# A hybrid recurrence and retention block: weight blocks stored in split form, a row moved to GpSimd's queue, and three orders changed

## The chip, the cores and the metric

The kernel runs on one core of one Trainium2 chip. The metric is the device time of one execution in microseconds (us). The core's engines are TensorE (PE in the rows; PEld is its weight load), VectorE (DVE), ScalarE (ACT) and GpSimd (POOL); SyncE (SP) issues most of the DMA transfers. Each engine works through its own queue in order; between the engines semaphores decide.

## The reference, cut to what matters

```python
T = concat(meta[16], x[4096])                     # 1024 wide
h = rmsnorm(T) * norm_gain
x_lru, gate, q, k, v, g = split(h @ w_in)         # 1024, 1024, 512, 512, 1024, 1024
y_lru = rg_lru(causal_conv(x_lru)) * gelu(gate)   # block-diagonal gates, linear scan over time
y_ret = head_norm(retention(rope(q), rope(k), v)) * silu(g)   # 8 heads, chunks of 128
out = rmsnorm(x + concat(y_lru, y_ret) @ w_out) * final_gain  # 4096 x 1024
```

All of it is float32.

## The kernel before, in words

Every float32 operand of a product is split into two float32r parts, hi and lo (`split`, L109 to L112: hi by a pass on ACT, L111, lo by a subtraction on DVE, L112), and a product is three matmuls, hi\*hi, hi\*lo and lo\*hi (`mm3`, L119 to L121). TensorE so has most of the work. The program goes through three parts, and a framework orders each engine's queue from the dependences and a simulated time line of its own: an edit of the program text so moves rows on every engine.

**The LRU part (to about 860 us).** Two passes, one for each half of the channels, each over 9 tiles of time (272, 256, then seven of 512). For a tile, four channel blocks each take two projections, `px` and `pg` (PSUM banks a and b, two buffers each). `block_front` (L544) multiplies px by the row 1/rms, which has been spread over the partitions as the tile `rb` (L553), then convolves and splits. `block_back` (L566) computes two gate products `pgt`, and at L576 `sg = pg * rb`: this reads pg and so frees its PSUM buffer. `sg` has 5 buffers (L574). `tail` (L594) scans, multiplies into sg, and stores sg to DRAM (`ydram`, L606, one store for each 128 positions of time): when that store has landed, the sg buffer is free again. The row 1/rms: `stats` (L486) computes it position by position (POOL rows L76 and L77), and from the third tile of the first pass on the result goes to DRAM as `rrow` (L493, 512 elements of 4 bytes) and comes back as rb (`load_rb`, L511); both are requests on SP's queue. The split x is kept in DRAM as `xs` for the later parts.

**The retention (823 to 2084 us).** Two passes over 32 chunks of 128 positions, each with four of the eight heads. `ret_x(ph, n)` (L166; loads L181) requests a chunk's xhi and xlo into the pool `big` (28 buffers), `front_qk` and `front_v` project, `back_s` and `back_o` compute the chunk's output (scores times mask `sm`, L845; `po` is the output's PSUM tile, L857; `on` its normed copy by ACT, L884). In the second pass `stage_w` (L196) prepares the output weights: for each of 8 row pairs of w_out it forms seven combinations (blocks 1 to 7) and stores each to DRAM (`put`, the tensors `wst`, 256 KB per transfer).

**The out-projection (from 2084 us).** Two sweeps (h = 0 for the LRU half of w_out, h = 1 for the retention half) over 16 pairs of row tiles. A pair (a `Unit`) needs seven products instead of eight, in the order of `ORDER` (L231): blocks 1, 6, 7, 5, 2, 4, 3, into PSUM banks a, b, c, d, a, c, d. `out_w(h, i, g)` (L233) loads a half of a block of weights into a tile of the pool `raws` (6 buffers) and splits it. `operand` forms and splits a pair's inputs (`yraw`, `yop`). `combine` (L311) reads the products: for block 1 ACT copies oa to `u` (L315), for block 7 `h1 = u + oc` (L321), and so on. The first two units run together. In the second sweep `finished` (L358) adds the first sweep's result to h by an accumulating load (L368, on POOL's queue); `added` (L398) then requests the squares for the last RMSNorm on ACT (L386, placed behind an instruction called `mark`) and the root on POOL (L393, L395), and `end` (L406) scales (L412) and stores the rows (L414). The last unit has its own end, `last_tile` (L371).

Of the kernel before, what the change touches and what calls it, by code (L numbers as in the profile page):

```python
# [17 lines left out]
P = 128  # L18
D = 1024
# [14 lines left out]
def hybrid_kernel(ctx: ExitStack, tc: tile.TileContext, xa, x, meta, w_in, w_out,  # L34
# [132 lines left out]
    def ret_x(ph, n):  # L167
        if (ph, n) not in rxs:
# [22 lines left out]

    wst = [[[dpool.tile([P, 2, 512], F32, name=f"wst{h}_{i}_{g}") for g in range(2)] for i in range(8)]
           for h in range(2)]
    hdram = [dpool.tile([P, D], F32, name=f"hdram{n}") for n in range(NT)]

    def stage_w(h, k):  # L196
        r = []
        for kk in (k, k + 4):
            t = raws.tile([P, 2, 512], F32, tag="raw", name="sraw")
            r0 = (8 * h + kk) * P  # L200
            nc.sync.dma_start(out=t, in_=w_out[r0:r0 + P, :].rearrange("p (c d) -> p c d", c=2))
            nc.scalar.activation(t, t, AF.Identity, scale=wsc[:, 8 * h + kk:8 * h + kk + 1])
            r.append(t)
        (b11, b12), (b21, b22) = [(t[:, 0], t[:, 1]) for t in r]

        def put(i, src):
            store.dma_start(out=wst[h][i][k // 2][:, k % 2, :], in_=src)

        put(1, b11)
        put(2, b21)  # L210
        put(3, b22)
        nc.vector.tensor_tensor(b11, b12, b11, op=ALU.subtract)
        put(5, b11)
        nc.vector.tensor_tensor(b12, b22, b12, op=ALU.subtract)
        put(7, b12)
        nc.vector.tensor_tensor(b22, b22, b11, op=ALU.subtract)
        put(6, b22)
        nc.vector.tensor_tensor(b21, b21, b22, op=ALU.subtract)
        put(4, b21)
# [13 lines left out]
    def out_w(h, i, g):  # L233
        if (h, i, g) not in wo:
            raw = raws.tile([P, 2, 512], F32, tag="raw", name="oraw")
            load(raw, wst[h][i][g])
            pool = xwp if i in (3, 4) or (i, g) == (2, 1) else big
            hi = pool.tile([P, 2, 512], F32R, tag="b", name="owh")
            lo = pool.tile([P, 2, 512], F32R, tag="b", name="owl")
            split(raw, hi, lo)  # L240
            wo[h, i, g] = (hi, lo)
        return wo[h, i, g]
# [68 lines left out]
    def combine(u, i):  # L311
        g = u.g
        if i == 1:
            u.u = osp.tile([P, 512], F32, name="u2")
            nc.scalar.copy(out=u.u, in_=g[0])  # L315
            return
# [8 lines left out]
        if late_unit(u):  # L325
# [9 lines left out]
            if i == 4:  # L335
                op = add(x1[:, :512], r1[:, :512], g[2])
                finished(u, 1, g[2])
            else:
                for c in range(2):
                    op = add(x0[:, 512 + 256 * c:768 + 256 * c], r0[:, 512 + 256 * c:768 + 256 * c],  # L340
                             g[3][:, 256 * c:256 * c + 256])
                    square_last(u, c)
                with tc.issue_after(op.ins):
                    end()
                    last_tile(u)
            return op
# [23 lines left out]

    def last_tile(u):  # L371
        t, n, v = u.x[0], u.n[0], u.r[0]
        nc.gpsimd.tensor_scalar(er[:, n:n + 1], es[:, n, 0:1], e2[:, 0:1], D * EPS, op0=ALU.add, op1=ALU.add)
        nc.gpsimd.tensor_tensor(er[:, n:n + 1], er[:, n:n + 1], e2[:, 1:2], op=ALU.add)
        nc.gpsimd.tensor_tensor(er[:, n:n + 1], er[:, n:n + 1], pm_half[:, 0:1], op=ALU.pow)
        nc.vector.tensor_tensor(v, t, gb, op=ALU.mult)
        nc.scalar.activation(v[:, :512], v[:, :512], AF.Identity, scale=er[:, n:n + 1])
        nc.sync.dma_start(out=out[n * P:(n + 1) * P, :512], in_=v[:, :512])
        nc.vector.tensor_scalar(v[:, 512:], v[:, 512:], er[:, n:n + 1], None, op0=ALU.mult)
        nc.sync.dma_start(out=out[n * P:(n + 1) * P, 512:], in_=v[:, 512:])  # L380

# [42 lines left out]
    def sweep():  # L424
# [7 lines left out]
        for s, (u, i, b) in enumerate(steps):  # L432
# [16 lines left out]
            if i == 7 or (i, u.n[0]) == (1, 4):  # L449
                added(u.hi[i], 2 if i == 1 else 0)  # L450
            if i in ((6, 5) if u.n[0] == 4 else (4,)) and not late_unit(u):
# [19 lines left out]
    with ExitStack() as ab:  # L471
# [14 lines left out]
        def stats(i):  # L486
# [5 lines left out]
            if i > 1:  # L492
                store.dma_start(out=rrow[i][0, :T].rearrange("(n p) -> p n", p=P),  # L493
                                in_=rstd[:, tiles[0]:tiles[-1] + 1])

        def load_rb(ph, i):
# [13 lines left out]
            else:  # L510
                nc.sync.dma_start(out=rb[:, :T],  # L511
                                  in_=rrow[i][:, :T].partition_broadcast(P).rearrange("a b c -> a (b c)"))
            return rb
# [52 lines left out]
        def block_back(ph, gw, st, T):  # L566
# [3 lines left out]
            for g in range(2):  # L570
                pgt = psp.tile([P, TB], F32, tag="cd"[g], name="pgt")
                mm3(pgt[:, :T], (gw[0][:, g, b, :], gw[1][:, g, b, :]), (xch[:, :T], xcl[:, :T]), True, True)
                ps.append(pgt)
            sg = tp.tile([P, TB], F32, tag="sg", name="sg", bufs=5)  # L574
            tg = mp.tile([P, TB], F32, tag="tg", name="tg", bufs=1)
# [134 lines left out]
    with ExitStack() as cd:  # L710
# [25 lines left out]
        for ph in range(2):  # L736
# [177 lines left out]
            vm = mv_  # L914
            front_v(cur)
            pkv = psp.tile([P, 2, 2, VD], F32, tag="d", name="pkvm")
            for h in range(4):
# [13 lines left out]
            for n in range(1, NT + 1):  # L931
# [25 lines left out]
                if n == NT - 1:  # L957
                    if ph == 0:
                        ret_x(1, 0)
                    else:  # L960
                        for g in range(2):
                            out_w(0, 7, g)
                back_o(prev)
# [94 lines left out]
```

## Time and profile before

| | |
|---|---|
| median of 3 runs | 2729.64 us (2727.87 to 2732.31) |
| the profiled execution | 2727.1 us |
| its span in the profile | 2725.3 us |
| TensorE busy in it | 2684.6 us (99%) |
| mean granted clock of TensorE | 0.995 |
| instructions | 36837 |

The span is what the profile covers of the execution; 1.8 us lie around it. TensorE leaves 40.7 us of the span idle, 9.5 us of them behind its last matmul. A timeline row reads: start, duration, engine, line, operation, output<-inputs, and in brackets the engine's idle time before it and what ended that. "x4" is the number of like instructions in the row; rows of one engine may overlap a little.

### The profile page before, as it was taken

Reading aid. Unit: us, or ns where it says so; the run is one execution under the profiler, and the core shown is the slowest. Engines: PE = TensorE matmul, PEld = TensorE weight load, DVE = VectorE, ACT = ScalarE, POOL = GpSimd, SP = SyncE. Lnnn points to the kernel's source line nnn. Section 1 sums busy time; section 2 is a strip of 40 time slices with the busy share of each in tenths; the row PEclk is TensorE's granted clock in tenths of the full one; section 3 lists DMA queues with packets and bytes.
Section 4 is the critical chain, followed back from the end, with each engine's and each line's share of the span. In section 5 each row is a group of like instructions: output and inputs, shape, how many; then the busy total and the mean of one; then the engine's idle time right before and its main releaser. Section 6 shows DMA issues by size and latency. Waiting matters only on the chain.

```text
span 2725.3 us, 36837 instructions
## 1 busy us (share of the span) xinstructions
PE 2684.6 (99%) x12950; PEld 2259.4 (83%) x12950; DVE 2047.0 (75%) x4553; ACT 1252.5 (46%) x2304; POOL 318.8 (12%) x619
## 2 busy tenths in 40 slices
PE   9999999999999999999999999999999999999998
PEld 8788889888887888888888888888887788887887
DVE  7787789676678877777779887888778755566665
ACT  7676667444454433333335444444334322244443
POOL 1010000000001111111111111111111101012222
PEclk9999999999999999999999999999999999999999
DMA  7765666423245333333335434444323745476664
GB/s 241 221 194 169 207 172 196 143 89 137 103 122 163 100 97 95 102 102 95 102 86 161 119 105 124 135 135 151 82 62 113 176 109 109 110 207 166 176 160 124
DMA packets 433695, 372.03 MB, mean 137 GB/s; under 512 B 160307, under 2 KB 363477, under 8 KB 432997
## 3 DMA queue, kind: packets, MB, share of 16 engines
q1 hardware_dynamic: 420260, 321.44, 38.8%
q0 software_dynamic: 13248, 48.24, 8.6%
q8 instruction: 101, 1.65, 0.3%
q14 instruction: 86, 0.70, 0.1%
HBM read 254.11 MB, written 132.27 MB: 142 GB/s over the span
## 4 chain that ended last, share of the span: by engine, by line
PE 81%; DVE 8%; DMA 6%; issue 2%; ACT 2%; SPq 1%; POOL 0%; POOLq 0%; DVEq 0%; ACTq 0%
PE ps L121 12%; PE ps L119 12%; PE ps L120 12%; PE px L120 3%; PE px L121 3%; PE pg L119 3%; PE pg L120 3%; PE pg L121 3%; PE px L119 3%; DMA ydram<-sg 3%; PE po L857 2%; PE od L308 2%; PE oc L308 2%; PE od L306 2%; PE od L307 2%
## 5 line engine op out<-in xcount | busy, mean ns | idle before, releaser
L121 PE MATMUL ps<-cwh,xlo 128*128 128x512 f32 x1536 | 600.0, 391 | 3.0 <-DMA xlo<-xs 3.0
L120 PE MATMUL ps<-cwl,xhi 128*128 128x512 f32 x1536 | 600.0, 391 | 0.0
L119 PE MATMUL ps<-cwh,xhi 128*128 128x512 f32 x1536 | 599.6, 390 | 0.0
L121 PEld LDWEIGHTS ps<-cwh,xlo 128*128 128x128 f32 x1536 | 288.8, 188 | 64.9 <-DMA xlo<-xs 3.4
L119 PEld LDWEIGHTS ps<-cwh,xhi 128*128 128x128 f32 x1536 | 289.1, 188 | 57.0
L120 PEld LDWEIGHTS ps<-cwl,xhi 128*128 128x128 f32 x1536 | 288.6, 188 | 56.2 <-issue 0.2
L725 DVE STREAM_TRANSPOSE pT<-rd 32x128 f32<-32x128 f32 x1024 | 310.1, 303 | 16.4
L119 PE MATMUL pg<-xhi,lwh 128*128 128x512 f32 (+2 forms) x576 | 212.2, 368 | 6.5 <-DVE sg L576 6.2
L119 PE MATMUL px<-xhi,lwh 128*128 128x512 f32 (+2 forms) x576 | 213.3, 370 | 3.1 <-DVE xlb L553 2.6
L120 PE MATMUL px<-xlo,lwh 128*128 128x512 f32 (+2 forms) x576 | 213.1, 370 | 2.2 <-DMA xlo<-xs 1.2
L121 PE MATMUL px<-xhi,lwl 128*128 128x512 f32 (+2 forms) x576 | 212.8, 370 | 0.2 <-DVE lwl L112 0.2
L121 PE MATMUL pg<-xhi,lwl 128*128 128x512 f32 (+2 forms) x576 | 211.5, 367 | 0.0
L120 PE MATMUL pg<-xlo,lwh 128*128 128x512 f32 (+2 forms) x576 | 211.5, 367 | 0.0
L111 ACT ACTIVATE yop<-yraw 128x512 fp32r<-128x512 f32 x192 | 117.9, 628 | 194.6 <-PE od L308 70.7
L112 DVE TENSOR_TENSOR yop<-yraw,yop 128x512 fp32r<-128x512 f32 x192 | 130.7, 688 | 68.1 <-ACT yop L111 66.4
L559 DVE SCALAR_TENSOR_TENSOR xc<-xlb,vec,xc 128x512 f32<-128x512 f32 (+2 forms) x216 | 149.0, 690 | 21.7 <-ACT xc L556 18.4
L884 ACT ACTIVATE on<-po,nb,rs 128x128 f32<-128x128 f32 x256 | 96.5, 458 | 141.6 <-POOL nb L881 141.6
L119 PEld LDWEIGHTS pg<-xhi,lwh 128*128 128x128 f32 x576 | 108.8, 189 | 25.6 <-DVE sg L576 7.6
L825 DVE SCALAR_TENSOR_TENSOR gs<-th,gs 128x512 f32<-128x512 f32 x64 | 44.2, 691 | 112.4 <-ACT gs L824 112.3
L120 PEld LDWEIGHTS px<-xlo,lwh 128*128 128x128 f32 x576 | 109.2, 190 | 22.9 <-DVE xlo L114 2.5
L119 PEld LDWEIGHTS px<-xhi,lwh 128*128 128x128 f32 x576 | 109.2, 190 | 22.0 <-issue 2.8
L121 PEld LDWEIGHTS px<-xhi,lwl 128*128 128x128 f32 x576 | 109.3, 190 | 18.9 <-DVE lwl L112 0.4
(218 smaller groups left out, 5743.1 us busy)
## 6 DMA issues: line engine op xcount, KB each, us to landing
xhi<-xs SPq DMA_DIRECT2D x92, 512.0 KB, 4.5
xlo<-xs SPq DMA_DIRECT2D x92, 512.0 KB, 5.5
xn<-in_x_dram SPq DMA_DIRECT2D x32, 512.0 KB, 5.3
ydram<-sg SPq DMA_DIRECT2D x256, 64.0 KB, 1.7
hdram<-in_x_dram SPq DMA_DIRECT2D x32, 512.0 KB
yret<-yt SPq DMA_DIRECT2D x256, 64.0 KB, 2.2
yraw<-ydram SPq DMA_DIRECT2D x32, 512.0 KB, 3.3
hdram<-h POOLq DMA_DIRECT2D x32, 512.0 KB, 5.5
```

The costliest lines, as they stand in the source:

```text
L111: hi_op[0] = nc.scalar.activation(hi, src, AF.Identity)
L112: return nc.vector.tensor_tensor(lo, src, hi.bitcast(F32), op=ALU.subtract)
L119: nc.tensor.matmul(ps, ah, bh, start=start, stop=False)
L120: nc.tensor.matmul(ps, ah, bl, start=False, stop=False)
L121: nc.tensor.matmul(ps, al, bh, start=False, stop=stop)
L306: nc.tensor.matmul(o, ah, bh, start=k == 0 and not more, stop=False, skip_group_check=more)
L307: nc.tensor.matmul(o, ah, bl, start=False, stop=False, skip_group_check=more)
L308: mm = nc.tensor.matmul(o, al, bh, start=False, stop=k == 3, skip_group_check=more)
L559: conv = nc.vector.scalar_tensor_tensor(xc[:, :T], xl[:, j:j + T], vec[:, 6 + j, ch:ch + 1], xc[:, :T], op0=ALU.mult, op1=ALU.add)
L725: ins = nc.vector.transpose(dst[32 * g:32 * g + 32, :, 32 * q:32 * q + 32], sv[32 * q:32 * q + 32, :, g, :])
L857: nc.tensor.matmul(po[:, h, :], sm[:, h, :], v[:, h * VD:(h + 1) * VD], start=False, stop=(j == 1))
L884: nc.scalar.activation(on[:, h, :], po[:, h, :], AF.Identity, bias=nb[:, h:h + 1], scale=rs[:, h:h + 1])
```

## The change

Six edits.

1. Blocks 7 and 5 (`PRE`; the third and fourth products) are split in `stage_w` by a pass on ACT and one on DVE for each of 16 pieces of 128x512, and stored as hi and lo, 512 KB a store where it was 256 KB. `out_w` loads hi and lo of these blocks straight into the tiles of weights, so their 8 splits of 128x1024 in the sweeps go. At the last chunk of the retention the request for block 7's weights is joined by that for block 5's.
2. The store of `rrow` (7) and the loads of `rb` (16) go from SP's queue to POOL's.
3. `sg` has 6 buffers, not 5.
4. `ret_x(ph, 1)` is called earlier, ahead of the first chunk's kv product, in both passes.
5. In `added`, the mark behind which the first squares of the second sweep stand is the copy of u by ACT, not the split of the operand of block 1.
6. For the last unit the root of its second tile is computed with its own two instructions, r1 = x1\*gb and half of r0 = x0\*gb are formed before the last product is there, and the new `last_tiles` scales and stores both tiles (four stores on SP).

```diff
-    wst = [[[dpool.tile([P, 2, 512], F32, name=f"wst{h}_{i}_{g}") for g in range(2)] for i in range(8)]
+    PRE = (7, 5)
+    wst = [[[dpool.tile([P, 2 if i in PRE else 1, 2, 512], F32, name=f"wst{h}_{i}_{g}") for g in range(2)] for i in range(8)]
...
         def put(i, src):
-            store.dma_start(out=wst[h][i][k // 2][:, k % 2, :], in_=src)
+            dst = wst[h][i][k // 2][:, :, k % 2, :]
+            if i in PRE:
+                t = raws.tile([P, 2, 512], F32R, tag="raw", name="swp")
+                split(src, t[:, 0], t[:, 1])
+                store.dma_start(out=dst, in_=t.bitcast(F32))
+            else:
+                store.dma_start(out=dst[:, 0], in_=src)
...
     def out_w(h, i, g):
...
-            split(raw, hi, lo)
+            if i in PRE:
+                for s, t in enumerate((hi, lo)):
+                    load(t.bitcast(F32), w[:, s])
+            else:
+                raw = raws.tile([P, 2, 512], F32, tag="raw", name="oraw")
+                load(raw, w[:, 0])
+                split(raw, hi, lo)
...
-            nc.scalar.copy(out=u.u, in_=g[0])
+            u.cp = nc.scalar.copy(out=u.u, in_=g[0])
...
                 op = add(x1[:, :512], r1[:, :512], g[2])
-                finished(u, 1, g[2])
+                square(u, 1, 0, g[2])
+                q = er[:, u.n[1]:u.n[1] + 1]
+                nc.gpsimd.tensor_scalar(q, es[:, u.n[1], 0:1], es[:, u.n[1], 1:2], D * EPS, op0=ALU.add, op1=ALU.add)
+                nc.gpsimd.tensor_tensor(q, q, pm_half[:, 0:1], op=ALU.pow)
+                with tc.issue_after(op.ins):
+                    nc.vector.tensor_tensor(r1, x1, gb, op=ALU.mult)
+                    nc.vector.tensor_tensor(r0[:, :512], x0[:, :512], gb[:, :512], op=ALU.mult)
...
-                    end()
-                    last_tile(u)
+                    last_tiles(u)
...
+    def last_tiles(u):
+        n0, n1 = u.n
+        q0, q1 = er[:, n0:n0 + 1], er[:, n1:n1 + 1]
+        v0, v1 = u.r
+        nc.vector.tensor_tensor(v0[:, 512:], u.x[0][:, 512:], gb[:, 512:], op=ALU.mult)
+        nc.gpsimd.tensor_scalar(q0, es[:, n0, 0:1], e2[:, 0:1], D * EPS, op0=ALU.add, op1=ALU.add)
+        nc.gpsimd.tensor_tensor(q0, q0, e2[:, 1:2], op=ALU.add)
+        nc.gpsimd.tensor_tensor(q0, q0, pm_half[:, 0:1], op=ALU.pow)
+        for n, v, q in ((n1, v1, q1), (n0, v0, q0)):
+            nc.scalar.activation(v[:, :512], v[:, :512], AF.Identity, scale=q)
+            nc.sync.dma_start(out=out[n * P:(n + 1) * P, :512], in_=v[:, :512])
+            nc.vector.tensor_scalar(v[:, 512:], v[:, 512:], q, None, op0=ALU.mult)
+            nc.sync.dma_start(out=out[n * P:(n + 1) * P, 512:], in_=v[:, 512:])
...
-                added(u.hi[i], 2 if i == 1 else 0)
+                added(u.cp if u.n[0] == 4 else u.hi[i], 2 if i == 1 else 0)
...
-                store.dma_start(out=rrow[i][0, :T].rearrange("(n p) -> p n", p=P),
+                nc.gpsimd.dma_start(out=rrow[i][0, :T].rearrange("(n p) -> p n", p=P),
                                 in_=rstd[:, tiles[0]:tiles[-1] + 1])
...
-                nc.sync.dma_start(out=rb[:, :T],
+                nc.gpsimd.dma_start(out=rb[:, :T],
...
-            sg = tp.tile([P, TB], F32, tag="sg", name="sg", bufs=5)
+            sg = tp.tile([P, TB], F32, tag="sg", name="sg", bufs=6)
...
             front_v(cur)
+            ret_x(ph, 1)
...
-                        for g in range(2):
-                            out_w(0, 7, g)
+                        for i in (7, 5):
+                            for g in range(2):
+                                out_w(0, i, g)
```

The lists of instructions show what this does to the queues at three places. In the rows below a number behind a name tells one tile from another of that name; lines of the change are some 20 higher than those of before.

**The LRU part, DVE, second into third tile (about 67 to 77 us).** xlo_1216, xlo_1224 and xlo_1232 are pieces of the third tile's split x, sg_1185 and sg_1310 the third and the fourth sg of the second tile. Before:

```order
L114 SCALAR_TENSOR_TENSOR xlo_1216<-xraw_1213,vec_168,xhi_1215 128x512
L552 COPY xlb_1289<-hist_179 128x3
L598 TENSOR_TENSOR m_772<-m_772,t_771 128x272
L576 TENSOR_TENSOR sg_1185<-pg_1048,rb_860 128x256
L114 SCALAR_TENSOR_TENSOR xlo_1216<-xraw_1213,vec_168,xhi_1215 128x512
L114 SCALAR_TENSOR_TENSOR xlo_1224<-xraw_1221,vec_168,xhi_1223 128x512
L599 SCALAR_TENSOR_TENSOR t_771<-a_770,m_772 128x272
L114 SCALAR_TENSOR_TENSOR xlo_1224<-xraw_1221,vec_168,xhi_1223 128x512
L112 TENSOR_TENSOR xcl_1083<-xc_1077,xch_1082 128x256
```

With the change:

```order
L114 SCALAR_TENSOR_TENSOR xlo_1216<-xraw_1213,vec_168,xhi_1215 128x512
L596 TENSOR_TENSOR sg_1310<-pg_1139,rb_860 128x256
L572 COPY xlb_1289<-hist_179 128x3
L114 SCALAR_TENSOR_TENSOR xlo_1224<-xraw_1221,vec_168,xhi_1223 128x512
L618 TENSOR_TENSOR m_772<-m_772,t_771 128x272
L114 SCALAR_TENSOR_TENSOR xlo_1224<-xraw_1221,vec_168,xhi_1223 128x512
L112 TENSOR_TENSOR xcl_1083<-xc_1077,xch_1082 128x256
L114 SCALAR_TENSOR_TENSOR xlo_1232<-xraw_1229,vec_168,xhi_1231 128x512
```

sg_1185 has moved ahead of this piece (it is row 126 of the queue now, and was row 135), and about where it stood there is now sg_1310, the next one.

**The first two units, DVE (about 2102 to 2108 us).** sm_20878 and sm_20930 are the last chunk's masked scores, owl the lo parts of weights, yop operands of products. Before:

```order
L890 TENSOR_TENSOR on_20859<-on_20859,gs_20530 128x512
L112 TENSOR_TENSOR yop_21025<-yraw_20720,yop_21025 128x512
L845 TENSOR_TENSOR sm_20878<-pS_20871,msk_14404 128x512
L895 STREAM_TRANSPOSE yt_20925<-on_20859 128x512
L112 TENSOR_TENSOR owl_21031<-oraw_21028,owh_21030 128x1024
L112 TENSOR_TENSOR owl_21037<-oraw_21034,owh_21036 128x1024
L875 BN_STATS bs_20904<-po_20892 128x6 x4
```

With the change:

```order
L910 TENSOR_TENSOR on_20911<-on_20911,gs_20578 128x512
L112 TENSOR_TENSOR yop_21077<-yraw_20768,yop_21077 128x512
L915 STREAM_TRANSPOSE yt_20977<-on_20911 128x512
L112 TENSOR_TENSOR owl_21081<-oraw_21082,owh_21080 128x1024
L112 TENSOR_TENSOR yop_21132<-yraw_20775,yop_21132 128x512
L865 TENSOR_TENSOR sm_20930<-pS_20923,msk_14404 128x512
L895 BN_STATS bs_20956<-po_20944 128x6 x4
```

The two lo parts of block 5's weights are gone (owl_21031, owl_21037), and sm has moved behind the transpose, a lo part of block 2's weights and one operand.

**The second sweep's third unit, DVE (about 2457 to 2465 us).** h1_23245 and h1_23264 (23277 and 23296 in the change) are finished rows of the first two units, h1_23484 (23516) is the third unit's. Before:

```order
L318 TENSOR_TENSOR u2_23450<-u2_23450,ob_23435 128x512
L412 SCALAR_TENSOR_TENSOR h1_23245<-h1_23245,er_177,gb_21003 128x1024
L412 SCALAR_TENSOR_TENSOR h1_23264<-h1_23264,er_177,gb_21003 128x1024
L269 TENSOR_TENSOR yraw_23707<-yraw_23704,yraw_23707 128x512
L112 TENSOR_TENSOR yop_23506<-yraw_23404,yop_23506 128x512
L112 TENSOR_TENSOR yop_23526<-yraw_23407,yop_23526 128x512
L272 TENSOR_TENSOR yraw_23404<-yraw_23404 128x512
L321 TENSOR_TENSOR h1_23484<-u2_23450,oc_23436 128x512
```

With the change:

```order
L432 SCALAR_TENSOR_TENSOR h1_23277<-h1_23277,er_177,gb_21055 128x1024
L112 TENSOR_TENSOR yop_23538<-yraw_23436,yop_23538 128x512
L284 TENSOR_TENSOR yraw_23436<-yraw_23436 128x512
L112 TENSOR_TENSOR yop_23558<-yraw_23439,yop_23558 128x512
L432 SCALAR_TENSOR_TENSOR h1_23296<-h1_23296,er_177,gb_21055 128x1024
L112 TENSOR_TENSOR yop_23575<-yraw_23436,yop_23575 128x512
L333 TENSOR_TENSOR h1_23516<-u2_23482,oc_23468 128x512
```

The sum that reads oc, h1 = u + oc, still stands behind both scalings, which in the change are four rows apart.

## Rows read from the trace of the kernel before

**Rows 1.** The page's first part: busy time, share of the span and instructions.

```profile
PE 2684.6 (99%) x12950; PEld 2259.4 (83%) x12950; DVE 2047.0 (75%) x4553; ACT 1252.5 (46%) x2304; POOL 318.8 (12%) x619
```

**Rows 2.** Timeline of PE: the matmuls ahead of which it stood idle longest.

```profile
74.61 0.79 PE L119 MATMUL pg<-xhi,lwh 128*128 128x512 f32 x1 [4.15 <-DVE sg L576]
...
437.85 0.40 PE L119 MATMUL pg<-xhi,lwh 128*128 128x272 f32 x1 [1.57 <-DVE sg L576]
...
862.19 0.80 PE L121 MATMUL ps<-cwh,xlo 128*128 128x512 f32 x1 [3.00 <-DMA xlo<-xs]
...
2104.12 0.80 PE L306 MATMUL od<-owh,yop 128*128 128x512 f32 x1 [3.31 <-ACT owh L111]
...
2114.04 0.50 PE L306 MATMUL od<-owh,yop 128*128 128x512 f32 x1 [1.28 <-ACT on L884]
...
2455.48 0.67 PE L306 MATMUL oa<-owh,yop 128*128 128x512 f32 x1 [3.45 <-ACT u L315]
...
2464.52 0.50 PE L306 MATMUL oc<-owh,yop 128*128 128x512 f32 x1 [1.47 <-DVE h L321]
```

**Rows 3.** Busy time by stretch; the number behind POOL is TensorE's granted clock.

```profile
74.00:80.00 6.00, 5.39 (x14) 4.33 (x15) 5.87 (x13) 2.11 (x4) 0.00 (x0) 0.50 0.75 210
862.00:866.00 4.00, 3.81 (x11) 3.08 (x12) 3.79 (x10) 2.88 (x7) 0.46 (x1) 0.62 0.39 158
2098.00:2124.00 26.00, 17.51 (x74) 13.61 (x73) 19.17 (x35) 12.27 (x20) 4.48 (x8) 0.93 0.61 187
2456.00:2460.00 4.00, 4.00 (x13) 3.18 (x12) 3.97 (x5) 2.49 (x6) 1.63 (x2) 0.62 0.02 4
1498.00:2042.00 544.00, 544.00 (x2743) 463.29 (x2742) 436.74 (x1211) 224.39 (x466) 69.12 (x168) 1.00 0.39 114
```

**Rows 4.** The chain that ended last: start, us, what; one matmul at 80 us.

```profile
80.33 0.23 PE pg L119
```

**Rows 5.** Timeline of DVE in the LRU part.

```profile
74.13 0.42 DVE L576 TENSOR_TENSOR sg<-pg,rb 128x256 f32<-128x256 f32 x1 [5.75 <-DMA ydram<-sg]
...
83.78 0.68 DVE L553 TENSOR_TENSOR xlb<-px,rb 128x512 f32<-128x512 f32 x1
...
161.50 0.69 DVE L576 TENSOR_TENSOR sg<-pg,rb 128x512 f32<-128x512 f32 x1 [3.39 <-DMA ydram<-sg]
```

**Rows 6.** Timeline of SP: issues in the LRU part.

```profile
62.09 1.21 SPq L606 DMA_DIRECT2D ydram<-sg  x2
63.41 0.43 SPq L493 DMA_DIRECT2D rrow<-rstd  x1
...
74.69 0.32 SPq L511 DMA_DIRECT2D rb<-rrow  x1
...
150.41 2.08 SPq L606 DMA_DIRECT2D ydram<-sg  x4
```

**Rows 7.** The page's sixth part: issues, KB each, median us to landing.

```profile
ydram<-sg SPq DMA_DIRECT2D x256, 64.0 KB, 1.7
```

**Rows 8.** Timeline of SP: issues where the LRU part ends.

```profile
849.29 8.70 SPq L606 DMA_DIRECT2D ydram<-sg  x16
858.09 0.54 SPq L181 DMA_DIRECT2D xlo<-xs  x1
```

**Rows 9.** Timeline of DVE at the start of the out-projection.

```profile
2103.97 0.69 DVE L845 TENSOR_TENSOR sm<-pS,msk 128x512 f32<-128x512 f32 x1
...
2108.28 1.21 DVE L112 TENSOR_TENSOR owl<-oraw,owh 128x1024 fp32r<-128x1024 f32 x1
```

**Rows 10.** Timeline of ACT in the second sweep's third unit.

```profile
2453.48 0.60 ACT L386 ACTIVATE od<-h 128x512 f32<-128x512 f32 x1 [0.67 <-DMA h<-hdram]
...
2454.86 0.56 ACT L315 COPY u<-oa 128x512 f32<-128x512 f32 x1
```

**Rows 11.** Timeline of POOL: the roots of the last two tiles.

```profile
2715.13 0.56 POOL L395 TENSOR_TENSOR er<-er,pm_half 128x1 f32<-128x1 f32 x1
...
2718.01 1.43 POOL L375 TENSOR_TENSOR er<-er,pm_half 128x1 f32<-128x1 f32 x1
```

More of the change, by code (lines that the diff above doesn't have):

```diff
@@ L234, in out_w @@
         if (h, i, g) not in wo:
-            raw = raws.tile([P, 2, 512], F32, tag="raw", name="oraw")
-            load(raw, wst[h][i][g])
+            w = wst[h][i][g]
             pool = xwp if i in (3, 4) or (i, g) == (2, 1) else big
@@ L369, in finished @@
             adding.append((u, j, u.mate.g[3 - j]))
[L371 to L380, printed above, removed]
+    def last_tiles(u):
[11 more added lines that the diff above has]
+            nc.sync.dma_start(out=out[n * P:(n + 1) * P, 512:], in_=v[:, 512:])
     adding = []
@@ L510, in load_rb @@
             else:
-                nc.sync.dma_start(out=rb[:, :T],
-                                  in_=rrow[i][:, :T].partition_broadcast(P).rearrange("a b c -> a (b c)"))
+                nc.gpsimd.dma_start(out=rb[:, :T],
+                                    in_=rrow[i][:, :T].partition_broadcast(P).rearrange("a b c -> a (b c)"))
             return rb
```

## The prediction, before the result was known

> **What bounds the kernel now.** The page's first part comes first: TensorE is busy for 2684.6 of the 2725.3 us of the span [rows 1]. So the kernel can gain from two things only: the 40.7 us in which TensorE stands idle, and the time in which it runs at a lower clock. The change touches no matmul, so I read next where TensorE waits: the timeline of PE gives seven matmuls with a wait that matters [rows 2], and the reader is to see in each the engine behind the arrow. Then the table by stretch [rows 3]: behind the waits of 3 us and more the granted clock is 0.50 to 0.62, that is, TensorE runs for some us at the lower of its two levels, 1.2 GHz, after it stood idle. What that costs is its busy time there times one minus the clock. For each wait I then read the queue of the engine that it names [rows 5, 6, 8, 9, 10], and the change's order of rows, which says who is late next.
>
> The profiled execution took 2727.1 us, 2.5 less than the median of the runs. The sum is made against 2727.1; the forecast adds the 2.5.
>
> **A. LRU part, 74 us (sixth sg buffer; rrow and rb on POOL).** TensorE waits 4.15 us for sg [rows 2]; sg waits 5.75 us for a ydram store to free its buffer [rows 5]. The clock is 0.50 for the next 5.39 busy us, 2.7 us lost [rows 3]. Together 6.85. The store went out at 62.09, just ahead of rrow at 63.41 [rows 6], and landed at 74.1, where such stores take 1.7 us in the median [rows 7]. Stores that went out right after the fourth rrow, at 150.41, were late too: sg waits for one until 161.50 [rows 5, 6]. So a ydram store beside rrow's 512 elements of 4 bytes takes about 11 us, and the sixth buffer by itself does not end the wait: in the change's order sg_1185 is done early, but sg_1310 stands where it stood and needs the very store that landed at 74.1. Behind it on DVE stand two lo parts, xlo_1224, which TensorE wants 24 matmuls after 67.1 us, at 0.23 us each [rows 4] that is 72.5. If the store still landed at 74.1, the fifth part would be there at 75.4, and the wait would only shrink to some 3 us. The gain therefore rests on the queue: on POOL's own queue rrow's elements need not stand ahead of or among the ydram stores. I take the store at about 72, a rest of 1.5 us and no low clock behind it: **-5.0**. Bounds: -6.85 (all gone) and 0 (the store as late as now).
>
> The Trainium skill speaks against this (DMA: Bandwidth & Descriptors, section "Issuing engines are not separate DMA queues"): transfers issued on different engines run on the same 16 DMA engines and interleave, and only the issue time is saved. By that the term is 0 and not -5.0. The stores at 150.41 neither bear it out nor refute it, since they shared a queue with rrow; no run of before shows rrow on another.
>
> The moved requests also load POOL's queue. What else stands there in the LRU part are the roots that feed rrow itself, so nobody else waits behind them. The third tile's rb is issued at 74.69 and first used at 83.78 [rows 5, 6], later tiles' have some 10 us; TensorE needs that product's result only about 20 us after 70 us, so an rb that is late by up to 5 us costs nothing.
>
> **B. 438 us (sixth sg buffer).** 1.57 us of wait [rows 2] without a fall of the clock: **-1.5**. The matmuls' order changes from 437 to 490 us, so the bounds are -3 and +3, a wait of either sign like that at 862.
>
> **C. 862 us (`ret_x` early).** TensorE waits 3.00 us [rows 2] for xlo of the chunk n = 2, whose request stands behind 16 ydram stores (8.70 us) on SP and goes out at 858.09 [rows 8]. The edit moves the request of n = 1 up, not this one: in the change's queue both xhi and xlo of n = 2 stand behind the same 16 stores, xhi first. xhi was ahead of them before. TensorE now wants xhi two matmuls before the place where it waits today, at about 858.7, and has it at about 862.3, as xlo today. So the wait stays, a bit longer: **+0.7**. Bounds: -4.4 (3.00 and 0.38 times 3.81 us [rows 3], if the stores go out sooner) and +2.
>
> **D. Start of the out-projection (split blocks).** From 2098 to 2124 TensorE is idle for 26.00 - 17.51 = 8.5 us, and loses 0.07 x 17.51 = 1.2 us by the clock [rows 3]. The 3.31 us for owh of block 5 [rows 2] go, since hi and lo are loaded as they are. But the next wait moves up: TensorE does block 5's 12 matmuls (2.7 us from 2100.8 on) and then needs the scores sm. These were done at 2104.7 [rows 9]; in the change they stand behind a transpose, a lo part of 1.21 us and an operand, about 2.3 us more, so at 2107.0, a wait of 3.5 us. The second unit's block 5 then waits for on as before, 2.2 us where it was 1.28. At that matmul, 2114.04 before, I get 2114.6: nothing gained yet. Behind it the gain comes: the operand yop_21132 is made before sm and not at 2109.4, so the raws tiles come free sooner, the next yraw, u's copy and the lo parts follow, and the two smaller waits (2.5 of the 8.5 us) go for the most part. **-2.2**; bounds -6 (sm in time) and +1.
>
> **E. Third unit of the second sweep (squares behind the copy).** ACT does u's copy at 2454.86, behind squares that wait for loads of h [rows 10]; TensorE waits 3.45 us for it, then 1.47 for h1, and loses 1.5 us by the clock (0.38 x 4.00) [rows 2, 3]: 6.4. With the copy first, the 3.45 goes. Then h1 is late. In the change a square that waits for the third load of h (2453.48 [rows 10]) stands ahead of the second half of the first row's square, and the two scalings stand ahead of h1 on DVE. I follow ACT's queue row by row, 0.75 us a square with its sum: the second unit's first row has its sum at 2458.7, its root waits on POOL for a neighbour's sum at 2460.1 and is there at 2461.0; scaling 1.24, an operand and h1 itself 0.69 each give 2463.6. TensorE comes to that product at 2459.1: a wait of 4.6 us, with 1.5 by the clock. Against 2464.52 for a matmul that is now six later: **-0.8**. Bounds: -4.5 (root and store in time) and +2 (the clock lower for longer).
>
> **F. The end.** The last root took 1.43 us beside a 128x1024 product on DVE, 0.56 us where DVE had none [rows 11]. The change makes that product earlier: **-0.9**; bounds -1 and +0.5 (four last stores on SP for two).
>
> **At nothing:** 16 pairs of passes and the larger stores of the split blocks in the retention. They are 16 x (0.60 + 0.69) = 21 us on ACT and DVE [rows 9, 10] over 544 us in which TensorE never waits, DVE is idle for 107 us and ACT for 320 [rows 3]. Bounds 0 and the second rival.
>
> Sum: -5.0 - 1.5 + 0.7 - 2.2 - 0.8 - 0.9 = -9.7, 2717.4 for the profiled execution, **2720 us** as a median.
>
> **The rivals.** *The ydram store beside rrow stays late*, by the rule cited under A or because rrow's small writes hold up the memory and not the queue. For it: the late stores land with rrow, not after a fixed delay. Against: stores behind it on one queue must. A is 0 then: 2725.
>
> *The puts push the retention's path (slower).* Each put sets two passes ahead of work that TensorE waits for, in the stretch from 1498 to 2042. Its price is a pass and, if the clock falls, as at 2456, 1.5 us: 2.2 each, all 16 give 35, so 2755; from the fifth on they outweigh the sum. Against it: the idle time of DVE and ACT there [rows 3]. For it: no row shows how much of that is ahead of the path.
>
> *The waits go altogether.* The sum with A, D, E and F at their lower bounds is -6.85 - 1.5 + 0.7 - 6 - 4.5 - 1 = -19: 2710.5. For it: the edits name exactly the three waits. Against: the order of rows under D and E.
>
> *The edits do not do what they say.* The rows move, the waits change hands, and the sum is within a us or two: 2729.
>
> A second rule speaks against POOL's queue (the Trainium skill, SBUF — State Buffer, section "SBUF: two separate sides"): while DVE holds the port that it shares with GpSimd, GpSimd cannot write the descriptors of its own transfers. A root of 1.43 us beside DVE's product [rows 11] agrees for an operation; for a transfer no run of before shows it. By its example of 2.5 us more for a transfer, an estimate from that page, rrow and rb would come 5 us later, which the slack under A takes.
>
> **How the numbers follow.** 0.2%, 5.5 us, is about what a measurement of this kernel can tell from no change. The sum as made: 0.52, most of it (0.46) faster by over that, 0.06 within. The store stays late: 0.20, half faster (0.10), half within. The waits go altogether: 0.10. No effect: 0.11, within. Puts: 0.07, slower. Faster 0.66, same 0.27, slower 0.07. The range 2708 to 2730 takes in the sum with its bounds, the late store and most of the no effect; it leaves out the puts, the better half of the best case and a part of the no effect, about 0.17.
>
> **What would show it.** A: DVE's sg without a wait on ydram over 2 us anywhere near 70 us, and PE's first matmul there without a gap; wrong if that gap is 3 us again, with ydram or xlo as its releaser. C: a wait of some 3.5 us for xhi near 862. D: no wait for owh, but one for sm of 3 us or more. E: no wait for u, one of 4 to 5 us for h. F: the last root at 0.6 us. Retention from 1498 to 2042: PE busy throughout; any wait there makes the second rival right.

## The result and the profile after

The changed kernel takes 2710.4 us in the median of 4 runs (2706.32 to 2712.07), the kernel before 2728.76 us in 4 runs on the same chip (2726.47 to 2732.31). The ratio is 0.9933, 95% interval 0.9921 to 0.9945: some 18 us faster. The forecast was 2720 us.

In the page's first part of the changed kernel TensorE is busy 7.7 us less than in [rows 1], in a span of 2707.4 us instead of 2725.3; TensorE's mean granted clock went from 0.995 to 0.997, and the time that a lower clock costs is counted as busy.

```profile
PE 2676.9 (99%) x12950; PEld 2256.7 (83%) x12950; DVE 2047.7 (76%) x4562; ACT 1255.3 (46%) x2313; POOL 330.4 (12%) x642
```

So 30.5 us of idle time are left of 40.7. The view of TensorE's waits (us in all, times, longest) names them:

```profile
PE px L120 <- DVE xlo L114: 6.4, 1, 6.4
PE od L318 <- ACT on L904: 4.2, 2, 2.1
PE ps L119 <- DMA xhi<-xs: 3.1, 1, 3.1
...
PE po L877 <- DVE sm L865: 1.4, 1, 1.4
PE pg L119 <- DVE sg L596: 1.3, 1, 1.3
PE oc L318 <- DVE h L333: 0.8, 1, 0.8
```

Against [rows 2]: the waits for owh (3.31) and for u in the second sweep (3.45) are gone, the wait of 4.15 us for sg is one of 6.4 us for xlo, and the wait of 3.00 us for xlo is one of 3.1 for xhi.

To see where the 17.9 us of the two spans come from, I cut both timelines of PE at instructions that both have: the first `pkvm` of each retention pass, the first product of the out-projection, the first matmul of the eighth, the seventeenth and the twenty-first product into `ob` (block 6, one for each unit), and the last matmul's end.

```
                                             before    after   difference   predicted
LRU part and into the retention (A, B)       843.80   839.19     -4.6        -6.5
first retention pass (C)                     637.17   636.86     -0.3        +0.7
second retention pass (puts)                 603.28   603.06     -0.2         0
start of the out-projection (D)              150.02   146.93     -3.1        -2.2
from there to the second sweep               174.08   174.08      0           0
its first units (E)                           81.34    73.44     -7.9        -0.8
the other units                              226.08   226.07      0           0
behind the last matmul (F)                     9.56     7.80     -1.8        -0.9
```

"The start of the out-projection" ends with the eighth `ob`, "from there to the second sweep" with the seventeenth, and "its first units" with the twenty-first. The long wait of the LRU part, 6.4 us, is where the one of 4.15 us was, among the third tile's first products. DVE's timeline of the changed kernel, and POOL's under it:

```profile
77.61 0.42 DVE L596 TENSOR_TENSOR sg<-pg,rb 128x256 f32<-128x256 f32 x1 [8.32 <-DMA ydram<-sg]
```

```profile
64.77 1.00 POOL L513 DMA_DIRECT2D rrow<-rstd  x1 [0.31 <-POOL rstd L77]
77.94 0.57 POOL L531 DMA_DIRECT2D rb<-rrow  x1 [12.17 <-issue]
```

In the table by stretch (its columns are those of [rows 3]) the clock falls behind that wait, and no longer at the start of the out-projection (0.93 before):

```profile
72.00:80.00 8.00, 1.59 (x5) 1.00 (x4) 2.39 (x6) 1.51 (x3) 0.57 (x1) 0.68 0.80 178
80.00:86.00 6.00, 6.00 (x27) 4.93 (x26) 5.93 (x16) 2.31 (x6) 0.00 (x0) 0.86 1.03 370
...
2092.00:2118.00 26.00, 19.80 (x93) 15.61 (x92) 18.73 (x34) 12.65 (x22) 3.98 (x8) 1.00 0.59 177
```

The idle 6.41 us and the clock's 0.32 x 1.59 + 0.14 x 6.00 = 1.35 make 7.8 where [rows 2, 3] gave 6.85. So A cost 0.9 us in this pair of profiles, and B is the rest of the first line, about -5.5.

### The profile page after: what moved, and what is told of

Same layout as the page of the kernel before. It is cut to its first block, busy times and chain, and to the rows that moved or that the text cites. A ratio compares the mean times of both kernels' runs of the same rounds, so it can differ in the third digit from the quotient of the medians.

```text
span 2707.4 us, 36911 instructions
## 1 busy us (share of the span) xinstructions
PE 2676.9 (99%) x12950; PEld 2256.7 (83%) x12950; DVE 2047.7 (76%) x4562; ACT 1255.3 (46%) x2313; POOL 330.4 (12%) x642
## 4 chain that ended last, share of the span: by engine, by line
PE 91%; DMA 3%; DVE 3%; ACT 1%; issue 1%; POOL 0%; SPq 0%; POOLq 0%; DVEq 0%; ACTq 0%
PE ps L120 12%; PE ps L119 12%; PE ps L121 12%; PE px L119 4%; PE px L121 4%; PE px L120 4%; PE pg L120 4%; PE pg L121 4%; PE pg L119 4%; PE po L877 2%; PE oc L318 2%; PE od L319 2%; PE od L320 2%; PE oc L319 2%; PE od L318 2%; PE oc L320 2%
## 5 line engine op out<-in xcount | busy, mean ns | idle before, releaser
L752 ACT CAST sbh<-state 64x256 fp32r<-64x256 f32 x128 | 51.9, 405 | 157.8 <-DVE state L889 151.1
```

## The experiments

Theory after the result: rrow's 512 small writes hold up the transfers beside them from any queue (A); the sixth sg buffer made B; the 8 us of E need both the new mark and the split blocks. The rivals are the queue for A and B, and one edit alone for E. Each ratio is to the kernel before on the same chip.

**The third tile's rb without rrow (A).**

```diff
-            if i > 1:
+            if i > 2:
                 nc.gpsimd.dma_start(out=rrow[i][0, :T].rearrange("(n p) -> p n", p=P),
...
-            if ph == 0 and i <= 1:
+            if ph == 0 and i <= 2:
```

> The changed kernel, where the third tile's rb is spread by four products on TensorE (as the first two tiles' are; about 0.27 us each) and so the rrow request of 64.8 us, with its 512 writes of 4 bytes, goes; rrow's store of that tile then follows as one row of 2 KB. The order on DVE near 70 us is the same. Theory (rrow's small writes hold up the ydram stores beside them): sg's wait of 8.3 us for ydram and TensorE's wait of 6.4 us near 78 us go but for 2 us at most, the clock stays high, 6 to 8 us less: about 2703 us. Rival (the loads of x and the stores of xs beside it hold the store up): TensorE still waits 4 us or more there, 2711 us.

Measured: 2700.33 us, ratio 0.9904 (0.9890 to 0.9917). The same row of DVE now waits 0.64 us, and TensorE's stretch has neither the gap nor the lower clock:

```profile
69.29 0.42 DVE L596 TENSOR_TENSOR sg<-pg,rb 128x256 f32<-128x256 f32 x1 [0.64 <-DMA ydram<-sg]
```

```profile
72.00:80.00 8.00, 8.00 (x45) 6.93 (x45) 6.72 (x18) 3.02 (x7) 0.00 (x0) 1.00 0.99 390
```

In those 8 us the DMA engines are counted as 0.99 busy and move 390 GB/s; in the changed kernel they were 0.80 busy at 178. The stall itself stands out from 70 to 76 us. The changed kernel, and then this run:

```profile
70.00:76.00 6.00, 2.41 (x12) 1.70 (x10) 0.00 (x0) 1.38 (x3) 0.00 (x0) 0.90 0.76 36
```

```profile
70.00:76.00 6.00, 6.00 (x31) 5.03 (x30) 5.93 (x14) 3.12 (x7) 0.00 (x0) 1.00 0.93 316
```

In the changed kernel the engines are counted as 0.76 busy and move 36 GB/s. They had begun packets that did not end: in each of the eleven profiles with the third tile's rrow, 20 to 35 packets of 4096 bytes from this stretch took over 1.5 us, the longest 3.9 to 6.5; in the three without it (this run and the last two below) none took over 1.4. So the delay sits in the transfers and not in a queue that they wait in. The store of ydram that went out last ahead of rrow, by its row of issues (KB each, us to landing), in the changed kernel and in this run:

```profile
ydram<-sg SPq DMA_DIRECT2D x1, 64.0 KB, 12.9
```

```profile
ydram<-sg SPq DMA_DIRECT2D x1, 64.0 KB, 6.0
```

Both are over the median of 1.7 [rows 7]: without rrow the store is still slow, but TensorE does not wait for it. The first `pkvm` comes at 831.86 instead of 839.19, 7.3 us sooner; the stall's 7.8 less the four products' 1.1 would be 6.7. The loads of x and the stores of xs are still there, so they are not what TensorE waited for: the rrow request was the cause.

**rrow and rb on SP again (A).**

```diff
-                nc.gpsimd.dma_start(out=rrow[i][0, :T].rearrange("(n p) -> p n", p=P),
+                store.dma_start(out=rrow[i][0, :T].rearrange("(n p) -> p n", p=P),
...
-                nc.gpsimd.dma_start(out=rb[:, :T],
+                nc.sync.dma_start(out=rb[:, :T],
```

> The changed kernel with rrow and rb on SP's queue again, all else kept. Theory (rrow's 512 writes of 4 bytes hold up the transfers beside them whichever queue they are in): the wait near 78 us stays, 4 to 7 us, and the time is 2710 us, 2 more or less. First rival (POOL's queue made that wait longer, from 4.15 to 6.41): the wait is 4 us or less, 2708 us. Second rival (rb behind the ydram stores of 464 to 476 us held up the stretch up to 490 us): waits there again, 2713 us or more.

Measured: 2710.95 us, ratio 0.9943 (0.9929 to 0.9958), not to be told from the changed kernel. The time is the theory's; the wait stays, but is shorter, as the first rival had it:

```profile
76.96 0.79 PE L120 MATMUL px<-xlo,lwh 128*128 128x512 f32 x1 [3.92 <-DVE xlo L114]
```

**The kernel before with only these two requests on POOL (A, B).** The same edit, the other way round, on the kernel before.

> The kernel before with rrow and rb on POOL's queue and nothing else. Theory (the queue does nothing for the wait near 75 us, since rrow's writes hold up the stores from any queue): 3 us or more for sg stay there, 2727 to 2729 us. Rival (as the prediction had it, the queue is what ends that wait): under 2 us there, 2723 us. Second rival (the queue alone takes the waits at 437 to 485 us away): none over 0.5 us there, 2724 us.

Measured: 2726.22 us, ratio 0.9990 (0.9981 to 0.9999). The wait near 75 us is longer, not shorter, and waits near 476 to 482 us remain, so both rivals are out:

```profile
76.66 0.79 PE L119 MATMUL pg<-xhi,lwh 128*128 128x512 f32 x1 [5.47 <-DVE sg L576]
...
481.73 0.50 PE L120 MATMUL px<-xlo,lwh 128*128 128x512 f32 x1 [0.91 <-DMA xlo<-xs]
```

Over all the profiles that have the third tile's rrow, those of before and of the change among them, TensorE's wait there was 3.92 to 4.83 us in the four with both requests on SP and 5.47 to 7.04 in the seven with them on POOL. So this edit made the wait of A longer, by 1.9 us between the two means.

**Five sg buffers again (B).**

```diff
-            sg = tp.tile([P, TB], F32, tag="sg", name="sg", bufs=6)
+            sg = tp.tile([P, TB], F32, tag="sg", name="sg", bufs=5)
```

> The changed kernel with 5 sg buffers again, all else kept. Theory (the sixth buffer gave the 4 to 5 us that TensorE gained between 437 and 490 us, and does nothing at 74 us): DVE's sg waits for ydram near 437 us again, TensorE's waits of 1 to 2 us near 437 to 485 us come back, about 2715 us; the wait near 78 us stays at 4 to 7 us. Rival (that gain came from taking rb and rrow off SP's queue): no such wait near 437 us, 2710 us.

Measured: 2712.43 us, ratio 0.9948 (0.9934 to 0.9961). Between theory and rival, and as a time not to be told from the changed kernel: no wait at 437 us, three of 0.40 to 0.74 us from 475 to 481, and the first `pkvm` at 840.75, 1.6 us later than in the changed kernel, 0.7 of it there by the first 39 us of the program.

**The sixth buffer alone, on the kernel before (B).** The same line with 6 for 5.

> The kernel before with a sixth sg buffer and nothing else. Theory (the buffer alone gives the 4.5 us that TensorE gained from 437 to 490 us): no wait there, 2724 us; the wait near 75 us stays at 4 us or more. Rival (buffer and queue must change together, or the queue alone does it): waits of some 3 us in all near 437 to 485 us, 2727 us or more.

Measured: 2723.43 us, ratio 0.9990 (0.9981 to 0.9999). Its first `pkvm` is at 838.58, 5.2 us sooner than in the profile of the kernel before; the ratio allows 0 to 5 us. The wait near 76 us is 4.79, and one of 0.62 is left at 462: the theory. The stretch from 430 to 460 us is that of the changed kernel. The kernel before, the sixth buffer alone, and the change, 430 to 460 us:

```profile
430.00:460.00 30.00, 27.60 (x211) 26.16 (x211) 26.83 (x67) 21.61 (x41) 1.50 (x2) 1.00 0.56 171
```

```profile
430.00:460.00 30.00, 30.00 (x246) 30.00 (x245) 27.62 (x67) 20.10 (x40) 0.00 (x0) 1.00 0.57 172
```

```profile
430.00:460.00 30.00, 30.00 (x246) 29.92 (x245) 27.50 (x68) 20.24 (x40) 0.58 (x1) 1.00 0.55 169
```

The idle 2.4 us go, and a matmul takes 30.00 / 246 = 0.122 us where it took 27.60 / 211 = 0.131: the kernel before also waited inside what is counted as busy.

All fourteen profiles together say more than a pair. From the first product of the fourth tile (behind the wait of A) to the first `pkvm`, the four with five buffers took 717.7 to 721.9 us and the ten with six 714.9 to 716.3. With six buffers it does not matter which queue rrow and rb are in: 715.5 to 716.0 on SP in three profiles, 714.9 to 716.3 on POOL in seven. (With five it is 719.2 and 721.9 on SP and 717.7 and 719.0 on POOL, too few to tell.) So the buffer made B, and by the means, 719.4 and 715.7, it is worth 3.8 us. The pair of before and after has 5.6 because the kernel before's profile is the longest of its four.

**The last LRU tile's stores on POOL (C).**

```diff
-                store.dma_start(out=ydram[n][:, ch, :], in_=sg[:, o + j * P:o + (j + 1) * P])
+                (nc.gpsimd if (ph, i) == (1, last) else store).dma_start(out=ydram[n][:, ch, :], in_=sg[:, o + j * P:o + (j + 1) * P])
```

> The changed kernel with the last LRU tile's ydram stores on POOL's queue. Theory (the wait of 3.1 us for xhi near 857 us stands behind 16 stores on SP's queue): the request for xhi goes out some 8 us earlier, no wait over 0.5 us there and no low clock behind it, 4 to 5 us less: about 2706 us. Rival (the transfers themselves are late, or the next wait takes over): a wait of 2 us or more stays near 857 us, 2710 us.

Measured: 2706.86 us, ratio 0.9927 (0.9914 to 0.9941). The wait is gone, and the first retention pass takes 632.76 us, 4.1 less: 632.2 to 632.8 in the three profiles with this edit, 635.6 to 639.2 in the other eleven. SP's queue in the changed kernel, and then in this run:

```profile
844.49 7.97 SPq L626 DMA_DIRECT2D ydram<-sg  x16
852.56 0.65 SPq L181 DMA_DIRECT2D xhi<-xs  x1
```

```profile
846.06 0.58 SPq L181 DMA_DIRECT2D xhi<-xs  x1
846.74 0.62 SPq L181 DMA_DIRECT2D xlo<-xs  x1
```

The stretch from 856 to 860 us in the changed kernel, and then in this run:

```profile
856.00:860.00 4.00, 3.23 (x8) 2.56 (x9) 3.07 (x8) 3.97 (x7) 0.22 (x1) 0.57 0.99 348
```

```profile
856.00:860.00 4.00, 4.00 (x20) 3.30 (x19) 3.85 (x12) 1.79 (x6) 2.16 (x6) 1.00 0.13 51
```

**Without the early request of x (C).**

```diff
             front_v(cur)
-            ret_x(ph, 1)
```

> The changed kernel without the early request of the second chunk's x. Theory (that edit does nothing for the wait near 857 us, whose request is the third chunk's): a wait of 2.5 to 4 us stays there, for xlo or xhi, 2709 to 2712 us. Rival (the early request shortens it): 5 us or more there, 2713 us.

Measured: 2710.71 us, ratio 0.9939 (0.9927 to 0.9951): the edit is worth nothing that shows. The wait is 3.41 us, for xlo.

**Without the split blocks (D, E).**

```diff
-    PRE = (7, 5)
+    PRE = ()
...
-                        for i in (7, 5):
-                            for g in range(2):
-                                out_w(0, i, g)
+                        for g in range(2):
+                            out_w(0, 7, g)
```

> The changed kernel without split-form blocks (PRE empty, only block 7 requested early), all else kept. Theory (the split form is worth what the start of the out-projection gained, 3 us): TensorE waits 3 us for owh near 2097 us again, 2713.5 us. Rival (it also brings the sums of the first two rows pairs of the second sweep, and so the loads of h, forward, and a part of the 8 us gained near 2450 us is its own): the first load of h is issued 4 us later against TensorE's work, TensorE waits near 2445 to 2460 us for h or u, 2716 to 2721 us.

Measured: 2720.55 us, ratio 0.9978 (0.9969 to 0.9987). Both waits came, and the time is the rival's: the wait for owh is back (3.31), the start of the out-projection takes 150.46 us, and in the second sweep TensorE waits for h1, which the first units of that sweep pay with 78.53 us instead of 73.44:

```profile
2456.85 0.80 PE L318 MATMUL oc<-owh,yop 128*128 128x512 f32 x1 [3.32 <-DVE h L333]
```

The second retention pass takes 603.05 us without the puts' passes and 603.06 with them.

**The old mark (E).**

```diff
-                added(u.cp if u.n[0] == 4 else u.hi[i], 2 if i == 1 else 0)
+                added(u.hi[i], 2 if i == 1 else 0)
```

> The changed kernel with the squares of the second sweep's first rows placed behind the split of the operand again and not behind the copy of u. Theory (this edit alone gave the 8 us near 2450 us): TensorE waits 3 to 5 us for u again near 2440 to 2450 us, loses 1.5 us by the clock and waits for h, 2716 to 2718 us. Rival (the split blocks did it, which bring the loads of h forward): the squares find h landed, no wait over 1 us, 2710 to 2712 us.

Measured: 2715.62 us, ratio 0.9961 (0.9947 to 0.9975). Neither expectation came whole: no wait for u, but one of 2.86 us and one of 0.96 for h; the first units of the second sweep take 77.86 us.

**The new mark alone, on the kernel before (E).**

```diff
-            nc.scalar.copy(out=u.u, in_=g[0])
+            u.cp = nc.scalar.copy(out=u.u, in_=g[0])
...
-                added(u.hi[i], 2 if i == 1 else 0)
+                added(u.cp if u.n[0] == 4 else u.hi[i], 2 if i == 1 else 0)
```

> The kernel before with the squares placed behind the copy of u and nothing else. Theory (this edit and the split blocks give the 8 us near 2450 us together; alone it is what the prediction worked out): no wait for u there, but one for h of 3 to 5 us, 0 to 3 us less: 2725 to 2728 us. Rival (the edit alone does it): no wait over 1 us there, 2720 us.

Measured: 2725.23 us, ratio 0.9992 (0.9983 to 1.0000). No wait for u, one for h1:

```profile
2461.72 0.50 PE L306 MATMUL oc<-owh,yop 128*128 128x512 f32 x1 [3.03 <-DVE h L321]
```

The first units of the second sweep take 78.40 us. So from 81.34 the mark alone takes 2.9 us, the split blocks alone 3.5 (77.86 with the old mark) and both 7.9: it takes both, the theory. Without either, the three profiles have 80.0 to 82.6, and with both, the eight have 73.4 to 74.8. The two single gains make 6.4; that the edits do more together than apart is not shown, since the other 1.5 us is within that scatter.

**Both remaining stalls taken away.** The edits of the first run and of the run for C together.

> Both earlier edits together: the third tile's rb by products on TensorE, and the last LRU tile's ydram stores on POOL's queue. Theory (two separate stalls): neither the wait near 78 us nor the one near 857 us, 10 and 4 us less than the changed kernel, about 2696 us. Rival (the second stall is only passed on by the first): 2700 us as with the first edit alone.

Measured: 2697.64 us, ratio 0.9890 (0.9877 to 0.9903), with no wait over 2.5 us left. It beats both kernels.

**The same with rrow and rb on SP.**

> As the run with both earlier edits, with rrow and rb on SP's queue again. Theory (moving them to POOL gives nothing once no rrow stands beside stores that TensorE waits for): the same time within 2 us, no new wait over 1 us in the LRU part. Rival (rb behind blocks of ydram stores on SP holds up the second pass at 440 to 490 us): waits of 2 us or more there, 3 us more.

Measured: 2699.29 us, ratio 0.9895 (0.9883 to 0.9908), with no new wait over 1 us in the LRU part: the theory. Moving the two requests to POOL is worth nothing here that these runs can tell.

## Why the prediction was right, and where it was not

The direction and the range were right; the sum, -9.7 against -17.9, was not, and A failed outright. That the time still lies in the range, near its lower end, is in part luck: half of the forecast gain was A's and did not come, while B and E together gave some 11 us more than forecast. The 2710.4 us are also the figure of the third rival (*The waits go altogether*, 2710.5), but not its case: the wait of A became longer, and those for sm and on are there.

**A, predicted -5.0, measured +0.9.** The step that failed: "on POOL's own queue rrow's elements need not stand ahead of or among the ydram stores". On POOL's queue the store was as late as on SP's, and the wait longer; only without the request did it go. This is the first rival, which had a chance of 0.20. The rule of the Trainium skill cited there (DMA: Bandwidth & Descriptors, section "Issuing engines are not separate DMA queues") would have given the better term, 0; the waits of 5.47 to 7.04 us on POOL agree with it. The prediction's own sign came, a gap of over 3 us with xlo as its releaser. Why the waits are longer on POOL than on SP is open. The second rule of the Trainium skill cited (SBUF — State Buffer, section "SBUF: two separate sides"), on GpSimd's descriptors, would make rrow itself later, by an estimate from its example 2.5 us. The traces show little of that: rrow landed 11.2 to 12.5 us after its issue on SP (four profiles) and 11.9 to 13.0 on POOL (seven), 0.7 later in the mean. Another difference is in the traces: on SP the load of rb, which waits for rrow, holds back what stands behind it, and the kernel before issues one store of 512 KB between the two; in the changed kernel SP issues five transfers of that size from 67.44 to 72.03, into the stall. That this lengthens the wait was not tried. Nor was it that it is the size of 4 bytes, and not something else in that request. (The rrow ahead of the stores of 150.41 is the third of these requests, not the fourth.)

**B, predicted -1.5, measured about -5.5 in this pair, 3.8 by the means of all profiles.** The mechanism was right, the term mis-sized. I took the one wait of 1.57 us in [rows 2] as the whole price; the stretch from 368 to 490 us had 4.3 us of idle time in the kernel before and 1.3 in the change, and slower matmuls beside. A part of the pair's figure is chance: the run with the new mark alone, whose LRU part is that of before, had no wait at 437 us and reached the first `pkvm` 2.4 us sooner.

**C, predicted +0.7, measured -0.3.** As the prediction had it: the wait stays, for xhi, with 16 stores ahead of the request, and the run with those stores on another queue shows that they are its cause. SP issues the 16 in 7.97 us, one behind the other, 0.5 us each; so here, other than in A, it is the queue that delays the neighbour.

**D, predicted -2.2, measured -3.1.** The wait for owh goes and one for sm takes its place, but of 1.37 us and not 3.5. Two waits of 2.1 us for on stand around it, where one of 2.2 was predicted. Of the nine profiles with split blocks that of the changed kernel alone shows the first of the two at this length; in seven of the others this stretch took 144.2 to 144.8 us. Against 150.0 to 151.3 in the five without, split blocks are usually worth 5 to 7 us here, around the bound of -6.

**E, predicted -0.8, measured -7.9.** The step that failed: "In the change a square that waits for the third load of h (2453.48 [rows 10]) stands ahead of the second half of the first row's square". The order was read rightly, but the load's time, 2453.48, was taken from the kernel before. In the change POOL issues the first of these loads 13.6 us sooner, where TensorE is only 8.2 ahead. Before, and then after:

```profile
2440.71 0.88 POOL L368 DMA_DIRECT2D h<-hdram  x1 [32.61 <-DVE h L322]
```

```profile
2427.12 0.89 POOL L385 DMA_DIRECT2D h<-hdram  x1 [30.18 <-DVE h L334]
```

ACT's copy of u then stands ahead of all the squares, these follow while TensorE has work, and h1 is there without a wait. ACT and DVE after:

```profile
2435.68 0.59 ACT L327 COPY u<-oa 128x512 f32<-128x512 f32 x1 [2.03 <-PE oa L320]
...
2440.63 0.60 ACT L406 ACTIVATE od<-h 128x512 f32<-128x512 f32 x1 [3.22 <-DMA h<-hdram]
...
2449.28 0.59 ACT L327 COPY u<-oa 128x512 f32<-128x512 f32 x1 [2.09 <-PE oa L320]
```

```profile
2449.03 0.68 DVE L333 TENSOR_TENSOR h<-u,oc 128x512 f32<-128x512 f32 x1
```

The split blocks had been counted for the first sweep's start alone. They take the same passes out of the second sweep's start too. That they bring the loads of h forward is shown by the run without them, with the new mark:

```profile
2434.98 0.89 POOL L385 DMA_DIRECT2D h<-hdram  x1 [32.34 <-DVE h L334]
```

That is 7.9 us later, where TensorE is 2.7 behind. That run and the one with the mark alone show what I had worked out: a wait of 3.3 and 3.0 us for h1 (predicted 4.6) in place of that for u.

**F, predicted -0.9, measured -1.8.** The last root took 0.56 us instead of 1.43, as forecast:

```profile
2702.41 0.56 POOL L395 TENSOR_TENSOR er<-er,pm_half 128x1 f32<-128x1 f32 x1
```

The rest is not settled: the span behind the last matmul was 7.7 to 7.8 us in six of the ten profiles with the new end and 8.5 to 10.3 in the others; with the old end it was 9.6 in three and 8.1 in one.

**At nothing.** The puts cost nothing, and the second rival is out: TensorE is busy for all of the 544 us in the change too:

```profile
1498.00:2042.00 544.00, 544.00 (x2742) 463.28 (x2741) 443.38 (x1225) 232.16 (x479) 68.95 (x169) 1.00 0.41 120
```

## What to carry to other kernels

Before a request is moved to another queue because it delays its neighbours, ask whether the queue or the transfer does it: leave it out once and look at the neighbour. Here it was the transfer in A and the queue in C. A term that rests on the change's order needs the change's times as well: where an edit takes work out of an early place, follow the loads and sums behind it to every later place that uses the same buffers. And a row of a wait gives only the wait of that row; the gain of a buffer is read from the whole stretch, idle time and time per matmul.

## What the runs showed that I had not expected

One request of 512 elements of 4 bytes, of 2 KB in all, cost TensorE 7.8 us in the changed kernel: from its issue at 64.77 to 77.94 us the load of rb behind it waited, and a store of 64 KB on the other queue, issued 0.23 us ahead of it, landed as late. Nearly the same code also differs from profile to profile by more than some of these effects: the first retention pass, which most of the edits don't touch, took 635.6 to 639.2 us in the runs that kept its wait, so a single profile does not tell 1 or 2 us there.
